# Gate build: a pair of PSUM buffers for each side's bit products, the j side's shared with the run-ahead products

## The chip, the cores and the metric

One core of a Trainium2 chip runs the whole program. The metric is the time of one execution in microseconds on the device, as the median of several runs.

## The reference

A two-layer backbone over 512 latent tokens and 256 context tokens, width 1024. Each layer has an attention part (mLSTM and differential attention in layer 0, windowed attention in layer 1) and then PEER, which is what this case is about: for each token and each of 8 heads, two lists of 128 scores are made, the 16 best of each are paired, the 16 best pairs pick 16 of 16384 single-neuron experts, and the token's output is the sum over the picked experts.

```python
s = jnp.einsum('nhpd,hpkd->nhpk', q, keys)
sv, si = lax.top_k(s, PEER_TOPK)                       # 16 best of 128, for both halves p
cand = sv[:, :, 0, :, None] + sv[:, :, 1, None, :]
cidx = si[:, :, 0, :, None] * PEER_NKEYS + si[:, :, 1, None, :]
cs, ci = lax.top_k(cand.reshape(n, PEER_HEADS, -1), PEER_TOPK)
gate = jax.nn.softmax(cs, axis=-1)
a = jnp.einsum('nd,nhkd->nhk', xt, u[eidx])
w = gate * jax.nn.gelu(a, approximate=False)
return jnp.einsum('nhk,nhkd->nd', w, v[eidx])
```

## The kernel before

PEER is done in two ways at once. For the three first blocks of 128 latent tokens (384 tokens) it is dense: a matrix of gates G[token, expert], zero where an expert is not picked, is built and stored to memory (`gd`). Then a loop over 128 slices `j` of 128 experts makes A = u x^T (tile `dA`), z = gelu(A) G and adds z^T v into six PSUM banks (`dacc`). For the other blocks (the fourth latent one, and the context's two) the picked rows of u and v are fetched by indirect DMA, one expert per token and step, and worked on by VectorE (lines 1023 and 1036). These gather steps are issued beside the dense work.

The stage around the change is the first half of `peer` (the block under `self.mixing()`), once in each layer:
- `route` makes queries (`pqps`) and scores (`pss`) on TensorE; `select` (lines 924 to 1001) finds the best pairs, a chain of many small VectorE instructions with steps on GpSimd (line 980) and ScalarE between them, for four blocks.
- After each of the first three blocks `gate_build` (from line 1062) runs: VectorE cuts the expert numbers i and j into bits (lines 1073 and 1075), which go through memory (`bd`) to come back transposed (`gbits`). Then 32 units per block, 96 per layer, one for every four tokens. `front`: two TensorE products of the bits, `gds` (line 1091), one for the i side and one for the j side, each in a PSUM bank of its own, are 1 exactly where all bits agree; ScalarE's Relu makes `ghot` of the i side (line 1097), VectorE's max and multiplication by the gate makes `ghot` of the j side (line 1095). `back`: four fp32 products `gps` (line 1108; eight records in the profile) make G for four tokens, and after two units ScalarE copies them to `gch` (line 1110). `pipe` calls `front` of a unit ahead of `back` of the one before.
- In layer 0, `mod(1, [0, 1])` makes two modulation rows for layer 1: 128 products `modps` (line 252), read by VectorE (lines 353 to 356).
- Then the first `dA` tiles of the dense loop run ahead, 18 in layer 0 and 27 in layer 1, with 24 products each (line 217). Their weights are split into a rounded and a remaining part: `whi` on ScalarE and `wlo` (line 196) on GpSimd and VectorE in turn. From the dense phase on the same work has the names `dhi` and `dlo`.

In layer 0, 48 gather steps belong to this stage (`GROWS`), three for every five units from the 17th on.

PSUM is divided among three tags with two buffers each: `pj` (`pqps`, `modps`, `dA` and others), `po` (`pss`, `gtp`, `gds`) of one bank a buffer, `big` (`gps`) of two. A buffer is given out in the order in which the program asks, and a user of it waits until the last readers of the buffer's previous user are done. The order of instructions on each engine is made by a scheduler when the program is built; it may put an instruction ahead of others that come earlier in the program, as far as the buffers allow it.

Of the kernel before, what the change touches and what calls it, by code (L numbers as in the profile page):

```python
# [110 lines left out]
class Kern:  # L111
# [951 lines left out]
    def gate_build(self, b, sel, alloc, beside):  # L1063

        nc, wk = self.nc, self.wk
        _, g, fij, _ = sel
        pl = alloc().bitcast(BF16).rearrange("p (e x) -> p e x", e=8)
        nc.gpsimd.memset(pl[:, 7, :], 1.0)  # L1070
        for s in range(2):
            bu = alloc().bitcast(U32).rearrange("p (e x) -> p e x", e=8)
            nc.vector.tensor_copy(bu[:, 7, :], fij[:, 128 * s:128 * s + 128])
            for e in range(7):
                nc.vector.tensor_scalar(bu[:, e, :], bu[:, 7, :], 1 << e, None, op0=OP.bitwise_and)
            nc.scalar.copy(pl[:, 0:7, 128 * s:128 * s + 128], bu[:, 0:7, :])
        nc.sync.dma_start(self.bd[b].rearrange("(t e) x -> t e x", e=8), pl)
        pt = self.po([128, 128], "gtp")
        nc.tensor.transpose(pt, g, self.ident)
        gT = wk.tile([128, 128], F32, name="gT", tag="gT", bufs=2)  # L1080
        nc.scalar.copy(gT, pt)
        bits, G, ps = {}, {}, {}

        def front(u):
            c, t0 = u
            if c % 4 == 0 and t0 == 0:
                bits[0] = wk.tile([128, 4, 256], BF16, name="gbits", tag="gbits", bufs=2)
                nc.sync.dma_start(bits[0], self.bd[b].rearrange("(c p) x -> p c x", p=128)[:, c:c + 4, :])
            d = [self.po([128, 4, 128], "gds") for _ in range(2)]
            for s in range(2):  # L1090
                nc.tensor.matmul(d[s], bits[0][:, c % 4, 128 * s:128 * s + 128], self.gB[:, t0:t0 + 4, :],  # L1091
                                 start=True, stop=True)
            h = [wk.tile([128, 4, 128], F32, name="ghot", tag="ghot", bufs=6) for _ in range(2)]
            t = 16 * c + t0
            i = nc.vector.scalar_tensor_tensor(h[1], d[1], 0.0, gT[:, t:t + 4].unsqueeze(2).broadcast_to([128, 4, 128]),
                                               op0=OP.max, op1=OP.mult)
            nc.scalar.activation(h[0], d[0], AF.Relu)
            return h + [i]

        def back(u, h):  # L1100
            c, t0 = u
            if t0 == 0:
                G[0] = wk.tile([128, 128, 16], F32, name="gch", tag="gch", bufs=2)
            if t0 % 8 == 0:
                ps[0] = self.big([128, 8, 128], "gps")
            beside(h[2])
            for t in range(4):
                nc.tensor.matmul(ps[0][:, t0 % 8 + t, :], h[0][:, t, :], h[1][:, t, :], start=True, stop=True)  # L1108
            if t0 % 8:
                nc.scalar.copy(G[0][:, :, t0 - 4:t0 + 4], ps[0].rearrange("p t j -> p j t"))  # L1110
            if t0 == 12:
                nc.scalar.dma_start(self.gd[8 * b + c], G[0])

        self.pipe([(c, t0) for c in range(8) for t0 in range(0, 16, 4)], front, back)

    def halves(self, src, shape, eng):
# [432 lines left out]
```

## Time and profile before

| | us |
|---|---|
| median of 3 runs | 4182.2 |
| lowest and highest | 4175.84, 4185.61 |
| the profiled execution | 4186.29 |
| its span in the trace | 4184.5 |

All times of the trace count from the start of the span. The stage of the change lies from 1099.8 (the last `pqps` product starts) to 1385.9 (the dense phase's first product) in layer 0, and from 2940 to 3215.8 in layer 1. Where a product stands in a timeline with "x8", eight of them are drawn together; TensorE's records overlap, so the rate is read from starts, not from durations.

### The profile page before, as it was taken

The numbers are of one execution on the slowest core, as the hardware profiler recorded it, in microseconds if no ns is written. First come the engines' busy times: TensorE is split into PE (matmuls) and PEld (weight loads), VectorE is DVE, ScalarE is ACT, GpSimd is POOL, SyncE is SP. The second block draws the span as 40 slices with busy tenths as digits, with TensorE's granted clock in tenths as the row PEclk, the third lists the DMA queues.
The fourth block names the chain that finished last, engine by engine and source line by source line (L and its number), as shares of the span: only waits on it lengthen the run. The fifth ranks groups of instructions, "written<-read, shape, count | busy, mean of one in ns | idle before, by whom it ended". The sixth has DMA issues, their size and how long they took to land.

```text
span 4184.5 us, 56313 instructions
## 1 busy us (share of the span) xinstructions
PE 3808.1 (91%) x19774; PEld 3252.5 (78%) x19780; DVE 3281.6 (78%) x5763; ACT 1526.5 (36%) x2798; POOL 2266.9 (54%) x1644
## 2 busy tenths in 40 slices
PE   8988777758899899999999889999999999999999
PEld 5776554546687799999889777777887899999987
DVE  4259888977988899999989987537955977777788
ACT  3322322412156433333333324332366333333333
POOL 1016767554453588778778563004531766666664
PEclk9999988878999999999999999999999999999999
DMA  5556888786339999989899995423346978788778
GB/s 193 171 201 207 314 316 308 263 314 234 129 121 371 361 326 346 350 310 343 317 332 331 341 332 194 154 90 112 117 161 241 347 275 285 275 288 278 280 266 314
DMA packets 389674, 1099.30 MB, mean 263 GB/s; under 512 B 32959, under 2 KB 140807, under 8 KB 383246
## 3 DMA queue, kind: packets, MB, share of 16 engines
q0 software_dynamic: 147456, 536.94, 35.4%
q1 hardware_dynamic: 232142, 497.95, 34.8%
q10 hardware_dynamic: 9792, 60.82, 3.5%
q8 instruction: 155, 2.54, 0.2%
q14 instruction: 129, 1.06, 0.1%
HBM read 1024.18 MB, written 71.40 MB: 262 GB/s over the span
## 4 chain that ended last, share of the span: by engine, by line
PE 55%; DMA 14%; DVE 13%; issue 10%; POOL 7%; ACT 2%; SPq 0%; POOLq 0%; ACTq 0%; DVEq 0%
PE dacc L1178 19%; PE dA L217 17%; DMA uv<-in_pr_u_dram,ix 4%; POOL uv L1010 4%; DMA uv<-in_pr_v_dram,ix 3%; PE pqps L217 2%; DMA draw<-in_uT_dram 2%; PE ops L223 2%; PE gps L1108 2%; DVE junkv L1023 2%; PE oo L1335 1%; PE gds L1091 1%; PE ops L1305 1%; PE modps L252 1%; PE vps L223 1%
## 5 line engine op out<-in xcount | busy, mean ns | idle before, releaser
L1178 PE MATMUL dacc<-dhi,dw 128*128 128x512 f32 x3072 | 986.6, 391 | 5.6 <-ACT dw L1171 3.8
L1010 POOL DMA_INDIRECT uv<-in_pr_u_dram,ix x512 | 670.2, 1309 | 463.0 <-DVE pa L1023 330.4
L1010 POOL DMA_INDIRECT uv<-in_pr_v_dram,ix x512 | 684.1, 1336 | 399.6 <-DVE pacc L1036 274.3
L1023 DVE CUSTOM_DVE_ANT_0 junkv<-uv,x 128x1024 bf16<-128x1024 f32 x512 | 695.1, 1358 | 60.1 <-DMA uv<-in_pr_u_dram,ix 55.9
L1036 DVE SCALAR_TENSOR_TENSOR pacc<-uv,pw,pacc 128x1024 f32<-128x1024 f32 x508 | 701.3, 1381 | 42.0 <-DMA uv<-in_pr_v_dram,ix 38.1
L1178 PEld LDWEIGHTS dacc<-dhi,dw 128*128 128x128 f32 x3072 | 578.5, 188 | 122.5 <-ACT dw L1171 4.5
L1123 POOL TENSOR_TENSOR dlo<-draw,dhi 128x1024 fp32r<-128x1024 f32 x210 | 542.3, 2583 | 211.4 <-ACT dhi L1122 207.7
L1122 ACT CAST dhi<-draw 128x1024 fp32r<-128x1024 f32 x467 | 489.5, 1050 | 445.2 <-issue 176.1
L1178 PE MATMUL dacc<-dlo,dw 128*128 128x512 f32 x1536 | 603.9, 393 | 7.2 <-DVE dlo L1123 7.2
L1168 DVE TENSOR_TENSOR dz<-dz,dG 128x384 f32<-128x384 f32 x256 | 406.5, 1601 | 79.0 <-ACT dz L1138 75.1
L1171 ACT CAST dw<-dz 128x384 fp32r<-128x384 f32 x256 | 131.4, 514 | 708.2 <-PE dacc L1178 690.3
L217 PE MATMUL dA<-xth,dhi 128*128 128x384 f32 x1688 | 335.3, 340 | 11.6 <-ACT dhi L1122 9.8
L1123 DVE TENSOR_TENSOR dlo<-draw,dhi 128x1024 fp32r<-128x1024 f32 x257 | 322.2, 1254 | 27.5 <-ACT dhi L1122 26.7
L1178 PEld LDWEIGHTS dacc<-dlo,dw 128*128 128x128 f32 x1536 | 289.1, 188 | 66.2 <-DVE dlo L1123 9.7
L217 PEld LDWEIGHTS dA<-xth,dhi 128*128 128x128 f32 x1688 | 306.5, 189 | 28.7 <-ACT dhi L1122 10.2
L217 PE MATMUL dA<-xtl,dhi 128*128 128x384 f32 x1688 | 327.4, 335 | 0.0
L217 PE MATMUL dA<-xth,dlo 128*128 128x384 f32 x1688 | 326.6, 334 | 0.8 <-POOL dlo L1123 0.8
L217 PEld LDWEIGHTS dA<-xtl,dhi 128*128 128x128 f32 x1688 | 296.7, 188 | 0.1
L217 PEld LDWEIGHTS dA<-xth,dlo 128*128 128x128 f32 x1688 | 295.6, 188 | 1.2 <-POOL dlo L1123 1.1
L1172 DVE TENSOR_TENSOR dw<-dz,dw 128x384 fp32r<-128x384 f32 x256 | 162.8, 636 | 151.5 <-ACT dw L1171 151.5
L1108 PEld LDWEIGHTS gps<-ghot 128*128 128x128 f32 x1536 | 202.2, 192 | 49.9 <-issue 21.9
L196 POOL TENSOR_TENSOR wlo<-wraw,whi 128x1024 fp32r<-128x1024 f32 x55 | 132.9, 2418 | 194.7 <-ACT whi L195 121.3
(341 smaller groups left out, 6044.9 us busy)
## 6 DMA issues: line engine op xcount, KB each, us to landing
draw<-in_pr_v_dram SPq DMA_DIRECT2D x256, 512.0 KB
draw<-in_uT_dram SPq DMA_DIRECT2D x211, 512.0 KB
wraw<-in_wb_dram SPq DMA_DIRECT2D x150, 512.0 KB
gd<-gch ACTq DMA_DIRECT2D x48, 1024.0 KB
dG<-gd SPq DMA_DIRECT2D x30, 1536.0 KB
wraw<-in_mod_t_dram SPq DMA_DIRECT2D x48, 512.0 KB
wraw<-in_uT_dram SPq DMA_DIRECT2D x45, 512.0 KB
wraw<-in_mod_w_dram SPq DMA_DIRECT2D x32, 512.0 KB
```

The source lines that it names most:

```text
L196: eng.tensor_tensor(lo, raw, hi.bitcast(F32), op=OP.subtract)
L217: self.nc.tensor.matmul(ps, w[wi][:, k, :], x[xi][:, k, 0:T], start=(i == 0), stop=(i == 23))
L1010: nc.gpsimd.indirect_dma_start(out=t, out_offset=None, in_=a[table], in_offset=bass.IndirectOffsetOnAxis(ap=ix[:, c:c + 1], axis=0))
L1023: nc.vector.tensor_tensor_reduce(out=junk, in0=u, in1=x, op0=OP.mult, op1=OP.add, scale=1.0, scalar=0.0, accum_out=A[:, c:c + 1])
L1036: nc.vector.scalar_tensor_tensor(acc, v, W[:, c:c + 1], acc, op0=OP.mult, op1=OP.add)
L1108: nc.tensor.matmul(ps[0][:, t0 % 8 + t, :], h[0][:, t, :], h[1][:, t, :], start=True, stop=True)
L1122: nc.scalar.copy(hi, raw)
L1123: eng.tensor_tensor(lo, raw, hi.bitcast(F32), op=OP.subtract)
L1168: nc.vector.tensor_tensor(z3, z3, self.G[:, :, j % JG, :], op=OP.mult)
L1171: nc.scalar.copy(wh, z)
L1172: i = nc.vector.tensor_tensor(wl, z, wh.bitcast(F32), op=OP.subtract)
L1178: self.nc.tensor.matmul(acc[b][:, h, :], w[wi][:, 128 * b:128 * b + 128], v[vi][:, 512 * h:512 * h + 512], start=(j == 0 and i == 0), stop ...
```

## The change

One line of `front`. Both `gds` of a unit came from the tag `po`, so a unit held both of its buffers. Now the i side's (`d[0]`) comes from `po` and the j side's (`d[1]`) from `pj`, with two buffers for each side.

```diff
         def front(u):
             c, t0 = u
...
-            d = [self.po([128, 4, 128], "gds") for _ in range(2)]
+            d = [self.po([128, 4, 128], "gds"), self.pj([128, 4, 128], "gds")]
             for s in range(2):
                 nc.tensor.matmul(d[s], bits[0][:, c % 4, 128 * s:128 * s + 128], self.gB[:, t0:t0 + 4, :],
                                  start=True, stop=True)
```

No instruction is added or taken away, but the scheduler's order changes on all engines. On TensorE in layer 0, behind the last queries, stood before (`gtp` is the transposition of the gates of block 0):

```order
L884 MATMUL pss<-ky,pq 128x128 x4
L252 MATMUL modps<-wraw,sc 2x128 x104
L217 MATMUL dA<-xth,whi 128x384 x8
L217 MATMUL dA<-xtl,whi 128x384 x8
L1079 MATMUL gtp<-cst,dgt 128x128
L217 MATMUL dA<-xth,whi 128x384 x8
L217 MATMUL dA<-xtl,whi 128x384 x8
L217 MATMUL dA<-xth,wlo 128x384 x16
```

...and further down, where the first two units' `gds` stand among the products of the fifth and sixth tile:

```order
L217 MATMUL dA<-xtl,whi 128x384 x5
L217 MATMUL dA<-xth,wlo 128x384 x3
L1091 LDWEIGHTS gbits
L1091 MATMUL gds<-gB,gbits 128x512
L1091 LDWEIGHTS gbits
L1091 MATMUL gds<-gB,gbits 128x512
L217 MATMUL dA<-xth,wlo 128x384 x5
L217 MATMUL dA<-xtl,whi 128x384 x3
L217 MATMUL dA<-xth,wlo 128x384 x8
L1091 LDWEIGHTS gbits
L1091 MATMUL gds<-gB,gbits 128x512
L1091 LDWEIGHTS gbits
L1091 MATMUL gds<-gB,gbits 128x512
L1108 MATMUL gps<-ghot 128x128 x4
```

In the same place, behind the last scores, stands now:

```order
L884 MATMUL pss<-ky,pq 128x128 x8
L1079 MATMUL gtp<-cst,dgt 128x128
L1091 LDWEIGHTS gbits
L1091 MATMUL gds<-gB,gbits 128x512
L1091 LDWEIGHTS gbits
L1091 MATMUL gds<-gB,gbits 128x512
L1091 LDWEIGHTS gbits
L1091 MATMUL gds<-gB,gbits 128x512
L1091 LDWEIGHTS gbits
L1091 MATMUL gds<-gB,gbits 128x512
L1091 LDWEIGHTS gbits
L1091 MATMUL gds<-gB,gbits 128x512
L1108 MATMUL gps<-ghot 128x128 x4
```

The `modps` and the `dA` products are gone from there: the first unit's `gds` follow the last scores at once, and five `gds` stand ahead of the first `gps` instead of four. The run of units goes on to the end of the gate build, where TensorE's rows now are:

```order
L1091 MATMUL gds<-gB,gbits 128x512
L252 MATMUL modps<-wraw,sc 2x128 x13
L1108 MATMUL gps<-ghot 128x128 x12
L252 MATMUL modps<-wraw,sc 2x128 x3
L1108 MATMUL gps<-ghot 128x128 x4
L252 MATMUL modps<-wraw,sc 2x128 x112
L217 MATMUL dA<-xth,whi 128x384 x8
L217 MATMUL dA<-xtl,whi 128x384 x8
L217 MATMUL dA<-xth,whi 128x384 x8
```

Here follow all 128 `modps` and then all 432 `dA` products of the 18 tiles (before, behind the last `gps` of this layer came the first `dhi` product). In layer 1, 42 `dA` products stand between the last three units' `gps`, and 606 behind them.

On VectorE, in layer 0, at the first units, the rows were these before (924 to 992 are the selection's lines, 1073 and 1075 the bits of the next block):

```order
L981 TENSOR_REDUCE sel<-sel 128x64
L1095 SCALAR_TENSOR_TENSOR ghot<-gds,gT 128x512
L988 TENSOR_SCALAR fij<-sel 128x64
L989 TENSOR_SCALAR fij<-fij 128x64
L990 TENSOR_SCALAR fij<-fij 128x64
L991 SCALAR_TENSOR_TENSOR sel<-fij,sel 128x64
L1073 CAST sel<-fij 128x128
L992 TENSOR_TENSOR sel<-sel 128x64
L1075 TENSOR_SCALAR sel<-sel 128x128 x3
L977 TENSOR_TENSOR sel<-sel,cst 128x1024
L1075 TENSOR_SCALAR sel<-sel 128x128 x4
L196 TENSOR_TENSOR wlo<-wraw,whi 128x1024
L1095 SCALAR_TENSOR_TENSOR ghot<-gds,gT 128x512
```

And now, some ten units into the gate build, with two blocks still to be selected (1023 is the gather step, `x_3582` its block of tokens):

```order
L988 TENSOR_SCALAR fij<-sel 128x64
L1095 SCALAR_TENSOR_TENSOR ghot<-gds,gT 128x512
L989 TENSOR_SCALAR fij<-fij 128x64
L1095 SCALAR_TENSOR_TENSOR ghot<-gds,gT 128x512
L1023 ISA junkv,pa<-uv,x_3582 128x1024
L1023 ISA pa 128x1
L990 TENSOR_SCALAR fij<-fij 128x64
L1095 SCALAR_TENSOR_TENSOR ghot<-gds,gT 128x512
L1023 ISA junkv,pa<-uv,x_3582 128x1024
L1023 ISA pa 128x1
L991 SCALAR_TENSOR_TENSOR sel<-fij,sel 128x64
L1073 CAST sel<-fij 128x128
```

The `ghot` of the j side and the gather steps stand between the selection's steps, where there was one `ghot` for every ten or more of them; 56 of the 96 `ghot` of layer 0 stand ahead of the selection's last row (line 996), against 11 before, and 46 of layer 1, against 12. The `wlo` and the `mrow` rows (lines 196 and 353 to 356) stand behind the last `ghot` of the layer. On SyncE's queue the loads of `wraw` for `modps` and `dA` stand behind the last `gbits` load; before, they were spread over the stage.

## Rows read from the trace of the kernel before

**Rows 1.** Page, part 1: busy time, share of the span, instructions of each engine
```profile
PE 3808.1 (91%) x19774; PEld 3252.5 (78%) x19780; DVE 3281.6 (78%) x5763; ACT 1526.5 (36%) x2798; POOL 2266.9 (54%) x1644
```

**Rows 2.** Timeline of TensorE, end of the gate build, both layers: start, us, instructions, [idle before]
```profile
1377.46 1.13 PE L1108 MATMUL gps<-ghot 128*128 128x128 f32 x8 [0.40 <-DVE ghot L1095]
1385.85 2.93 PE L217 MATMUL dA<-xth,dhi 128*128 128x384 f32 x8 [7.26 <-ACT dhi L1122]
...
3212.12 1.16 PE L1108 MATMUL gps<-ghot 128*128 128x128 f32 x8 [0.28 <-ACT ghot L1097]
3215.82 2.93 PE L217 MATMUL dA<-xth,dhi 128*128 128x384 f32 x8 [2.54 <-ACT dhi L1122]
```

**Rows 3.** Busy time by stretch, all engines
```profile
core 0: us, PE busy (x) PEld busy (x) DVE busy (x) ACT busy (x) POOL busy (x), PEclk, DMA share, GB/s
1099.80:1159.00 59.20, 48.80 (x363) 39.54 (x363) 51.67 (x231) 9.28 (x16) 19.86 (x19) 0.97 0.53 172
1159.00:1378.70 219.70, 200.91 (x1304) 171.35 (x1305) 181.74 (x426) 135.27 (x211) 97.21 (x96) 0.99 0.71 266
2940.00:2996.00 56.00, 50.19 (x281) 48.84 (x280) 50.42 (x223) 17.84 (x29) 30.27 (x22) 0.97 0.31 98
2996.00:3213.30 217.30, 208.68 (x1347) 180.61 (x1348) 128.60 (x332) 141.52 (x222) 58.03 (x54) 0.98 0.49 183
```

**Rows 4.** Groups of TensorE, 1099.8 to 1378.7, then 2940 to 3213.3
```profile
L1091 PE MATMUL gds<-gB,gbits 128*128 128x512 bf16 x189 | 63.3, 378 | 14.8 <-DVE ghot L1095 9.3 <-ACT ghot L1097 3.8
L252 PE MATMUL modps<-wraw,sc 128*2 128x128 f32 x256 | 30.0, 275 | 5.3 <-DMA wraw<-in_mod_t_dram 4.2 <-DVE mrow L356 1.1
...
L1091 PE MATMUL gds<-gB,gbits 128*128 128x512 bf16 x189 | 64.6, 381 | 4.5 <-DVE ghot L1095 3.9
```

**Rows 5.** Timeline of TensorE: shortest unit; a free tile; two steady units
```profile
1249.26 0.61 PE L1091 MATMUL gds<-gB,gbits 128*128 128x512 bf16 x2
1250.59 0.59 PE L1091 MATMUL gds<-gB,gbits 128*128 128x512 bf16 x2
...
1408.83 1.55 PE L217 MATMUL dA<-xth,dhi 128*128 128x384 f32 x8
1412.99 0.39 PE L1178 MATMUL dacc<-dhi,dw 128*128 128x512 f32 x1
...
3206.60 1.05 PE L1108 MATMUL gps<-ghot 128*128 128x128 f32 x8
3209.47 1.05 PE L1108 MATMUL gps<-ghot 128*128 128x128 f32 x8
```

**Rows 6.** Timeline of VectorE, last step of the bits of block 0, both layers
```profile
1156.82 1.97 DVE L1075 TENSOR_SCALAR sel<-sel 128x128 uint32<-128x128 uint32 x14
...
2993.76 1.97 DVE L1075 TENSOR_SCALAR sel<-sel 128x128 uint32<-128x128 uint32 x14
```

**Rows 7.** The same stretches, line 196 (`wlo`) alone: VectorE busy, GpSimd busy
```profile
1099.80:1159.00 59.20, 2.41 (x2) 4.81 (x2) 0.97 0.53 172
1159.00:1378.70 219.70, 13.29 (x7) 17.71 (x7) 0.99 0.71 266
2940.00:2996.00 56.00, 9.28 (x6) 11.96 (x5) 0.97 0.31 98
2996.00:3213.30 217.30, 11.00 (x8) 19.34 (x8) 0.98 0.49 183
```

**Rows 8.** Groups of VectorE, 1099.8 to 1396
```profile
L1095 DVE SCALAR_TENSOR_TENSOR ghot<-gds,gT 128x512 f32<-128x512 f32 x96 | 65.9, 686 | 26.6 <-PE gds L1091 26.6
L1023 DVE CUSTOM_DVE_ANT_0 junkv<-uv,x 128x1024 bf16<-128x1024 f32 x48 | 58.3, 1215 | 2.1 <-DMA uv<-in_pr_u_dram,ix 2.1
L354 DVE TENSOR_TENSOR mrow<-mrow,mg 2x256 f32<-2x256 f32 x4 | 5.2, 1300 | 3.6 <-DMA mg<-in_norm_g_dram 3.6
```

**Rows 9.** Timeline of TensorE, layer 1, after a wait for VectorE
```profile
3021.05 0.57 PE L1091 MATMUL gds<-gB,gbits 128*128 128x512 bf16 x1 [2.29 <-DVE ghot L1095]
3021.41 1.91 PE L1108 MATMUL gps<-ghot 128*128 128x128 f32 x8
```

## The prediction

> **What bounds the kernel now.** I read the page first. TensorE is busy for 91% of the span, VectorE for 78% [rows 1]; so work that TensorE has to do later is paid for, unless it was idle then. The change touches one stage, which occurs once in each of the two layers: expert selection and the building of the gates, before the dense phase. I looked for the edges of that stage in TensorE's timeline. In layer 0 the last gate product (`gps`) starts at 1377.5 us and the dense phase's first product at 1385.9; in layer 1 they start at 3212.1 and 3215.8 [rows 2]. The busy times by stretch show what the stage is made of [rows 3]. While the selection runs (1099.8 to 1159 and 2940 to 2996) VectorE is busy 51.7 of 59.2 us and 50.4 of 56.0; this chain of small instructions sets the pace. TensorE is nearly as busy there, 48.8 and 50.2 us, but with other work: the `modps` products (layer 0 only) and the run-ahead `dA` products, which depend neither on the selection nor on the gates. In the rest of the stage both engines are busy, TensorE 200.9 of 219.7 us in layer 0 and 208.7 of 217.3 in layer 1, VectorE 181.7 and 128.6. So now VectorE's selection and TensorE's run-ahead products cover each other, and the gate build comes after with most of its units.
>
> **What the change does to that.** The j side's `gds` now takes its buffer from the tag `pj`, which `modps` and `dA` use too. A tag has two buffers, handed out in the order in which the program asks. The program asks for 96 `gds` buffers per layer before it asks for `modps` and `dA`. Before, these were the only users of `pj` after the scores, so they ran ahead; now each waits until all but the last two `gds` of the layer have been read. The order listing shows it: in layer 0 all 128 `modps` and 432 `dA` products stand behind the gate build, all but the first 16 behind its last row; in layer 1 606 of 648 `dA` stand behind the last `gps`. The gate build moves forward in exchange: 56 of the 96 `ghot` of layer 0 now stand before VectorE's last selection step (11 before), 46 in layer 1 (12 before). Nothing else on TensorE changes place.
>
> **The small gain that the diff names.** A pair of banks for each side lets TensorE write the next unit's `gds` while both reads of the last are still under way. What it can remove is TensorE's idle time ahead of `gds`, 14.8 us in layer 0 and 4.5 in layer 1 [rows 4]: 19 us in all at the most. In steady state two units take 2.87 us, from one `gps` to the next but one [rows 5], so 1.435 us each; I keep that price, and take no gain here beyond the ends of the gate build worked out next.
>
> **Layer 0, end of the gate build.** VectorE finished the bits of block 0 at 1156.82 + 1.97 = 1158.8 us [rows 6]. Ahead of that stood 2.4 us of `wlo` subtractions [rows 7] and the `mrow` work of `modps`, 5.2 us with 3.6 us of waiting for its loads [rows 8]; all of that moves behind, so the bits are ready some 11 us sooner, at 1148. From 1159 to the end VectorE had 181.7 us of work, of which 13.3 were `wlo` [rows 3, 7]; 168.5 us remain, among them the 96 `ghot` (65.9 us) and the 48 gather steps (58.3 us) [rows 8], whose number stays. How densely can VectorE do this? It ran at 51.7/59.2 = 0.87 in the selection alone. Full density is the lower bound, 1316; the 181.7/219.7 = 0.83 of the later stretch gives 1352. I take 0.87, because most of the work is again selection with fillers: 1148 + 194 = 1342, against 1378.6 (the last `gps` row's start and its 1.13 us): 37 us sooner.
>
> **Layer 0, what comes behind.** The `modps` products: 30.0 us of TensorE and 5.3 us idle for their loads and evictions [rows 4], 35 us; nothing else is left to fill those 5 us. The `dA` products: 18 tiles of 24. Without a neighbour 24 take 4.16 us, from the first of them to the first `dacc` behind [rows 5], so 75 us; the loads, casts and subtractions for a tile are spread over four engines and were hidden at this rate in the dense phase, which I assume here too. Layer 0 loses 35 + 75 - 37 = 73 us.
>
> **Layer 1.** No `modps` and no gather steps here. Bits of block 0: 2993.76 + 1.97 = 2995.7 [rows 6], less 9.3 us of `wlo` ahead of them [rows 7]: 2987. VectorE's work from there was 128.6 less 11.0 [rows 3, 7], 117.6 us, of which 96 `ghot` at 686 ns [rows 8] are 66. Up to its last selection step it has 51.6 us of selection and 46 `ghot` (31.6 us), 83 us, at 50.4/56.0 = 0.90 92 us: 3079. The remaining 50 units are TensorE's, 1.435 us each, 72 us: the gates end at 3151, against 3213.3, 62 us sooner. Then 606 `dA` at 4.16/24 us, 105 us. Layer 1 loses 43 us.
>
> **The gaps ahead of the dense phase.** TensorE stood idle 7.3 us ahead of the dense phase's first product in layer 0 and 2.5 in layer 1, for a cast that waits for its load [rows 2]. With the gates written out long before, and fewer transfers beside it, these loads can come earlier, or stay where they are if their buffers are freed by the last `dA`. Bounds: 0 and 10 us off; I take 8 off, since the DMA share falls from the 0.71 of layer 0's stretch [rows 3].
>
> **Sum.** 73 + 43 - 8 = 108 us. The profiled execution took 4186.3 us, its span 4184.5; the median of the runs is 4182.2, a tenth of a per cent less, and I add to the median: 4290 us.
>
> **The clock, row and rule.** In layer 1 TensorE waited 2.29 us for a `ghot`; the eight `gps` records behind it took 1.91 us instead of 1.05 [rows 5, 9], the lower of its two levels (1.2 and 2.4 GHz). Such waits will be common once TensorE has only gates to do during the selection. The Trainium skill, page "TensorE: Matmul & The Clock Gate", section "Why this matters for your kernels", says that idle gaps between matmul bursts make TensorE fall back to half clock; that speaks against this change. The row agrees. By the row alone I charge nothing in the sum, since a slow unit still fits between two `ghot` of the selection; by the rule taken for every unit of the selection it would be the rival below that costs 41 us more.
>
> **Rivals.**
> First, the other side: faster. If `modps` and `dA` found idle time again, or the gate build gained more than they lose, only the 19 us of idle time would count: about 4163. For that the gates of layer 0 would have to end 110 us sooner than now, at 1268; VectorE has 168.5 us of work after 1148 and could not be done before 1316. The order listing rules out the first way. 2 in 100. No change at all needs the same, 2 in 100.
> Second, a much smaller loss: VectorE without a wait (25 us in layer 0, 9 in layer 1), units at 1.33 us (the shortest distance from one pair of `gds` to the next [rows 5]; 5 us), both gaps gone (2 us more): about 4249; a few per cent of the rest of the loads hidden would bring it under 4240. For it speaks that `ghot` now fills VectorE's waits for GpSimd. 14 in 100 for less than 4240.
> Third, the clock: the 102 units that stand in the selection at 2.6 us instead of 1.44 (scaled by 1.91/1.05), where VectorE gives one about every 2.2 us in layer 0: 0.4 us each, 41 us, 4331. It decides from the point at which a unit at the low level is longer than VectorE's spacing. Together with VectorE at 0.83 (10 us in each layer) it leaves the range upward. 12 in 100 above 4335.
> Fourth, `dA` alone behind the gates runs at its loads and not at TensorE: at 5 us a tile, 45 tiles cost 38 us more, 4328. Against it: the same tiles ran at 4.16 us in the dense phase under more transfers. It lies within the range.
>
> **Range.** The forecast and what lies around it: 70 in 100, 4240 to 4335, which leaves 12 above and 18 below (14, 2 and 2). Faster by over 0.2% 0.02, within 0.2% (about what a measurement of this kernel can tell from no change, 8 us) 0.02, slower 0.96.
>
> **What the profile after would show.** In both layers no `dA` from the tag `pj` before the last few `gps`; TensorE's busy share in the selection down to a third or so; the last `gps` near 1342 in layer 0; then an unbroken run of some 35 us `modps` and 75 us `dA`; the dense phase from about 1455 (70 us later) and 110 us later in layer 1. Wrong would be the forecast if the gate build ended over 60 us sooner in layer 0, if `dA` ran in its gaps, or if the dense phase, unchanged in its order, became shorter by itself.

## The result and the profile after

The changed kernel took 4275.5 us (median of four runs, 4270.5 to 4279.4) and the kernel before 4180.5 (four runs): the ratio is 1.0223, 95% interval 1.0208 to 1.0238, 95 us more. Ratios, here and below, are those on record, worked out from single executions; they can differ by 0.1% from the quotient of the medians (here 1.0227). The forecast was 4290, its range 4240 to 4335.

The profiled execution took 4279.4 us with a span of 4277.6. The page's first part, against [rows 1]: no engine got noticeably more work, the shares fell.

```profile
PE 3812.9 (89%) x19744; PEld 3253.8 (76%) x19780; DVE 3262.2 (76%) x5763; ACT 1528.4 (36%) x2798; POOL 2237.2 (52%) x1644
```

TensorE is busy for 5 us more and the span is 93 us longer, so about 88 us of the loss are time in which TensorE now stands idle. Where, is seen in the busy times by stretch, with the columns of [rows 3]. The first three rows of layer 0 end where the first block's bits, the last gate product and the last `modps` end; in layer 1 the rows are selection alone, gate build, run-ahead tiles:

```profile
core 0: us, PE busy (x) PEld busy (x) DVE busy (x) ACT busy (x) POOL busy (x), PEclk, DMA share, GB/s
1099.80:1147.00 47.20, 6.03 (x24) 4.58 (x22) 40.94 (x225) 3.12 (x9) 14.57 (x16) 0.54 0.00 1
1147.00:1331.40 184.40, 150.89 (x977) 119.37 (x996) 170.25 (x421) 104.27 (x162) 76.45 (x90) 0.91 0.76 284
1331.40:1368.40 37.00, 27.52 (x226) 19.06 (x225) 4.54 (x11) 2.06 (x2) 0.00 (x0) 0.95 0.71 248
1368.40:1445.60 77.20, 75.14 (x433) 74.82 (x433) 11.93 (x9) 38.08 (x55) 21.47 (x9) 1.00 0.41 133
...
2995.40:3042.50 47.10, 4.89 (x19) 3.67 (x17) 41.79 (x220) 3.33 (x9) 15.59 (x17) 0.53 0.05 19
3042.50:3203.90 161.40, 144.00 (x990) 117.56 (x1009) 109.72 (x323) 107.72 (x168) 34.61 (x47) 0.97 0.48 188
3203.90:3311.80 107.90, 104.63 (x605) 104.31 (x603) 14.70 (x12) 51.97 (x77) 28.62 (x13) 1.00 0.41 136
```

TensorE worked 48.8 of the first 59.2 us before [rows 3]; now it has 6 us of work in 47. The work that it had there is found in the third and fourth row, where VectorE has almost nothing to do (4.5 of 37.0 and 11.9 of 77.2 us). The second row is the gate build, which now runs beside the selection. The timeline of TensorE at its end, layer 0 and then layer 1, answers to [rows 2]:

```profile
1330.28 1.16 PE L1108 MATMUL gps<-ghot 128*128 128x128 f32 x8
1331.37 1.91 PE L252 MATMUL modps<-wraw,sc 128*2 128x128 f32 x16
...
1340.70 7.36 PE L252 MATMUL modps<-wraw,sc 128*2 128x128 f32 x64 [2.48 <-DMA wraw<-in_mod_t_dram]
...
1363.36 3.65 PE L252 MATMUL modps<-wraw,sc 128*2 128x128 f32 x32 [1.70 <-DMA wraw<-in_mod_t_dram]
1368.37 1.66 PE L217 MATMUL dA<-xth,whi 128*128 128x384 f32 x8 [1.36 <-ACT whi L195]
...
1441.98 1.55 PE L217 MATMUL dA<-xth,wlo 128*128 128x384 f32 x8
1445.59 1.66 PE L217 MATMUL dA<-xth,dhi 128*128 128x384 f32 x8 [2.06 <-ACT dhi L1122]
...
3202.39 0.83 PE L1108 MATMUL gps<-ghot 128*128 128x128 f32 x6
...
3306.94 1.55 PE L217 MATMUL dA<-xth,wlo 128*128 128x384 f32 x8
3311.76 2.55 PE L217 MATMUL dA<-xth,dhi 128*128 128x384 f32 x8 [3.27 <-ACT dhi L1122]
```

After the last `gps` comes what used to run ahead of it: all but 16 of the 128 `modps`, with waits for their loads, then 18 `dA` tiles without a gap, then the dense phase's first product (`dhi`). In layer 1 the last `gps` stands at 3202.4 and the tiles end at 3308.5.

To compare kernels whose earlier parts start a few us apart, I measure the stage from the start of the last `pqps` product to the start of the first `dhi` product, and the dense phase from there to the start of the last `dacc`; each is a difference of two starts in TensorE's timeline of the profiled execution, in us. In the kernel before, that last `pqps` product starts at 1099.5 and 2939.9.

| | layer 0: last `gps` | stage | dense | layer 1: last `gps` | stage | dense |
|---|---|---|---|---|---|---|
| before | 278.8 | 286.4 | 1004.2 | 273.1 | 275.9 | 958.1 |
| after | 230.2 | 344.6 | 1001.2 | 207.8 | 316.4 | 955.3 |
| difference | -48.6 | +58.2 | -3.0 | -65.3 | +40.5 | -2.8 |

The four differences of stages and dense phases make +92.9 us; the spans differ by 93.1.

### The profile page after: what moved, and what is told of

Read it like the earlier page. It is cut to its first block, busy times and chain, and to the rows that moved or that the text cites. A ratio compares the mean times of both kernels' runs of the same rounds, so it can differ in the third digit from the quotient of the medians.

```text
span 4277.6 us, 56312 instructions
## 1 busy us (share of the span) xinstructions
PE 3812.9 (89%) x19744; PEld 3253.8 (76%) x19780; DVE 3262.2 (76%) x5763; ACT 1528.4 (36%) x2798; POOL 2237.2 (52%) x1644
## 4 chain that ended last, share of the span: by engine, by line
PE 57%; DVE 16%; DMA 11%; issue 8%; POOL 6%; ACT 1%; SPq 0%; POOLq 0%; ACTq 0%; DVEq 0%; another core or an unknown queue 0%
PE dA L217 20%; PE dacc L1178 18%; POOL uv L1010 4%; DMA uv<-in_pr_u_dram,ix 3%; PE ops L223 3%; DMA uv<-in_pr_v_dram,ix 2%; PE pqps L217 2%; DVE junkv L1023 2%; PE gps L1108 2%; DMA draw<-in_uT_dram 2%; PE modps L252 1%; PE oo L1335 1%; DVE ghot L1095 1%; DVE pacc L1036 1%; DVE dz L1168 1%
## 5 line engine op out<-in xcount | busy, mean ns | idle before, releaser
L1010 POOL DMA_INDIRECT uv<-in_pr_v_dram,ix x512 | 674.4, 1317 | 406.2 <-DVE pacc L1036 273.9
L1168 DVE TENSOR_TENSOR dz<-dz,dG 128x384 f32<-128x384 f32 x256 | 418.7, 1649 | 75.8 <-ACT dz L1138 75.8
```

The lines of the kernel that those rows point to most:

```text
L1010: nc.gpsimd.indirect_dma_start(out=t, out_offset=None, in_=a[table], in_offset=bass.IndirectOffsetOnAxis(ap=ix[:, c:c + 1], axis=0))
L1168: nc.vector.tensor_tensor(z3, z3, self.G[:, :, j % JG, :], op=OP.mult)
```

## The experiments

**Theory A** is the prediction's: the loss comes from the place in which the tag `pj` is handed out, which puts `modps` and `dA` behind the gate build, where they cover nothing. Its rivals B to E place it elsewhere or weigh a part of it differently; what each of them expects stands with each run. The questions were: is each layer's share what A says; does the loss follow the shared tag or the second pair; does it go when the same products are asked for earlier; and what is a run-ahead tile worth ahead of the gates and behind them.

### One layer at a time

The j side's `gds` come from `pj` in layer 0 only, or in layer 1 only (`1` in place of `0`):

```diff
-            d = [self.po([128, 4, 128], "gds"), self.pj([128, 4, 128], "gds")]
+            d = [self.po([128, 4, 128], "gds"), (self.pj if self.layer == 0 else self.po)([128, 4, 128], "gds")]
...
         upre = self.upre = UPRE[l]
+        self.layer = l
```

> The j side's gds take the tag pj in layer 0 alone. Theory A (order: the loss is the run-ahead products that now stand behind the gate build, less what the gate build ends sooner): the loss of layer 0 alone, 55 to 60 us, so 4236 us, plus or minus 6. Theory B (the gate build itself becomes slower, whatever happens to the run-ahead products: its VectorE part crowds the selection and TensorE falls to its lower clock): about half of the 95 us, in proportion to 96 units in each layer, 4228 us. Alone it doesn't tell them apart; with the next run it shows whether the two layers add up.

> The j side's gds take the tag pj in layer 1 alone. Theory A: 27 dA tiles (112 us) behind, gates some 62 us sooner, 40 us slower than before, 4220 us, plus or minus 6; together with the run for layer 0 it gives the 95 us. Theory B: as in layer 0, 47 us, 4228 us.

Layer 0 alone: 4227.4 us against 4181.9, ratio 1.0109 (1.0092 to 1.0126), 45.5 us. Layer 1 alone: 4219.4, 1.0093 (1.0076 to 1.0110), 37.5 us. Layer 1 is as A expected. Layer 0 lies below A's range and on B's figure, so the time alone decides nothing there. By the trace the changed stage of layer 0 is 53.6 us longer (340.0) and that of layer 1 41.2 (317.0), the unchanged ones 1.7 and 3.6 shorter; the stages bear A out, and what the time of the first run gives back lies outside them, in a dense phase of 997.3 us instead of 1004.2. Why it is shorter stays open. Together the two runs lose 83 us, 12 less than the changed kernel; the intervals of the three ratios allow that the layers simply add up (1.09% and 0.93% against 2.23%).

### Sharing without a second pair, and a second pair without sharing

Both sides from `pj`, so that a unit holds both buffers of the tag, as it did those of `po` before:

```diff
-            d = [self.po([128, 4, 128], "gds"), self.pj([128, 4, 128], "gds")]
+            d = [self.pj([128, 4, 128], "gds") for _ in range(2)]
```

> Both sides' gds take the tag pj, so there is one pair of buffers for a unit as before, and the sharing with the run-ahead products as after. Theory A: the order is that of the changed kernel, so the whole loss stays, 4275 us, and up to 10 us more since the second pair's run-ahead of gds is gone: 4275 to 4290 us. Theory B (it is the second pair that lets the gate build crowd the selection): most of the loss goes, 4180 to 4220 us.

4289.8 us, ratio 1.0264 (1.0247 to 1.0281). The whole loss is there without the second pair, and 14 us more (1.0264 against 1.0223), within A's range and far from B's. The groups of TensorE in the gate build of layer 0, first of this kernel (1091 to 1328 us), then of the changed one (1101 to 1331.4); behind the bar stand busy time, mean ns, then the idle time ahead and what ended it (18 of the 192 records of `gds` are missing from the trace of the changed kernel, so its busy times are not compared):

```profile
L1108 PE MATMUL gps<-ghot 128*128 128x128 f32 x768 | 105.5, 282 | 0.7 <-DVE ghot L1095 0.7
L1091 PE MATMUL gds<-gB,gbits 128*128 128x512 bf16 x192 | 68.6, 395 | 47.4 <-DVE ghot L1095 25.5 <-DMA gbits<-bd 15.2 <-ACT ghot L1097 4.9
```

```profile
L1108 PE MATMUL gps<-ghot 128*128 128x128 f32 x768 | 112.3, 294 | 21.9 <-DVE ghot L1095 20.7 <-ACT ghot L1097 0.5 <-ACT gch L1110 0.3
L1091 PE MATMUL gds<-gB,gbits 128*128 128x512 bf16 x174 | 57.5, 403 | 20.3 <-DMA gbits<-bd 15.4 <-ACT ghot L1097 1.8 <-DVE ghot L1095 1.5
```

With the order fixed, the second pair does what its words say: TensorE's wait ahead of `gds` for a `ghot` of VectorE falls from 25.5 to 1.5 us. But 20.7 us of waiting for `ghot` come up ahead of `gps` instead, since VectorE sets the pace; the last `gps` comes 4.8 us sooner in layer 0 and 7.4 in layer 1.

The other way round, the j side gets a tag of its own, for which the banks are freed by giving `gps` one-bank buffers (`gq`), with ScalarE's copy after every unit instead of every two:

```diff
-            d = [self.po([128, 4, 128], "gds"), self.pj([128, 4, 128], "gds")]
+            d = [self.po([128, 4, 128], "gds"), self.ps.tile([128, 4, 128], F32, name="gds", tag="pk", bufs=2)]
...
-            if t0 % 8 == 0:
-                ps[0] = self.big([128, 8, 128], "gps")
+            ps[0] = self.ps.tile([128, 4, 128], F32, name="gps", tag="gq", bufs=2)
...
-                nc.tensor.matmul(ps[0][:, t0 % 8 + t, :], h[0][:, t, :], h[1][:, t, :], start=True, stop=True)
-            if t0 % 8:
-                nc.scalar.copy(G[0][:, :, t0 - 4:t0 + 4], ps[0].rearrange("p t j -> p j t"))
+                nc.tensor.matmul(ps[0][:, t, :], h[0][:, t, :], h[1][:, t, :], start=True, stop=True)
+            nc.scalar.copy(G[0][:, :, t0:t0 + 4], ps[0].rearrange("p t j -> p j t"))
```

> The j side has its own pair of PSUM banks, shared with nothing; the room comes from gps, which here has one bank a unit instead of two banks for two units, so ScalarE copies G after every unit. Theory A: the run-ahead products stand again among the units, the loss goes: 4165 to 4190 us, since at most the 19 us of TensorE's idle time ahead of gds can be won. Theory B (the second pair makes the gate build slower): 4230 to 4275 us.

4160.4 us, ratio 0.9958 (0.9941 to 0.9975): the pair is there, the sharing is not, and the loss is gone. By the medians this kernel is 21 us faster than the one before, by the ratio 18, and faster than A expected (4165 to 4190). Its control has the `gps` edit alone, on the kernel before:

> The kernel before with one PSUM bank of gps for each unit and a copy of G after every unit, both sides' gds still in po, two banks unused: the part of e4_own_banks that is not the second pair. Theory A says that e4's gain of 21 us (4160 us) comes from the second pair, so this run is as fast as before, 4176 to 4192 us. Rival C: the smaller gps tiles are what gained there, 4160 to 4170 us.

4171.0 us (eleven runs), ratio 0.9977 (0.9968 to 0.9985). So 9 of the 21 us come from the one-bank `gps` buffers, more than A expected of them and just under what rival C did. The rest, 12 us by the medians and 8 by the ratios, would be the pair's; the two intervals overlap (0.9968 to 0.9975), so this part is not shown clear of noise. TensorE's group of `gps` in the kernel before (1099.8 to 1378.7 us), then the groups of the kernel with banks of its own, layer 0, 1098.8 to 1377 us:

```profile
L1108 PE MATMUL gps<-ghot 128*128 128x128 f32 x768 | 102.0, 276 | 0.7 <-DVE ghot L1095 0.6
```

```profile
L1107 PE MATMUL gps<-ghot 128*128 128x128 f32 x768 | 102.6, 282 | 6.3 <-ACT ghot L1097 2.3 <-ACT gch L1108 2.3 <-DVE ghot L1095 1.2
L1091 PE MATMUL gds<-gB,gbits 128*128 128x512 bf16 x192 | 60.0, 384 | 9.6 <-DVE ghot L1095 6.7 <-ACT ghot L1097 2.2 <-issue 0.4
```

Of the 14.8 us ahead of `gds` [rows 4] 9.6 are left, and 5.6 us more stand ahead of `gps` than before (0.7). The two waits together are as long as before. In the profiled execution, 29.7 us faster than that of before, the stages are 8.3 and 6.8 us shorter (278.1 and 269.1), mostly because the last `gps` comes 3.3 and 6.3 us sooner and the time from the start of the last `gps` to the dense phase in layer 0 shrank from 7.5 to 2.5. The dense phases are 7.0 and 4.0 shorter (997.2 and 954.1). Against the control's own profile (stages 283.9 and 268.9, dense phases 1001.5 and 954.2) what the pair adds in these two executions lies all in layer 0, 5.8 us in the stage and 4.2 in the dense phase; for the second I have no cause.

### The order mended by asking earlier

Tags as in the changed kernel, but the program now asks for `modps` and `dA` between the units. A step is one `dA` tile or one of the eight `modps` buffers (`mod_steps` is `mod` with a `yield` behind each); 13 steps of layer 0 (12 of layer 1) are asked for ahead of the first unit, then one at every fourth (third) unit:

```diff
+LEAD, EVERY = (13, 12), (4, 3)
...
         def front(u):
             c, t0 = u
+            self.fill()
...
+                def run_ahead():
+                    if l == 0:
+                        yield from self.mod_steps(1, [0, 1])
+                    for j in range(upre):
...
+                        z[j] = self.dense_u(j, u, self.pj([128, ND], "dA"), xt)
+                        yield
+                work, units = run_ahead(), [0]
+                def fill():
+                    for _ in range(LEAD[l] if units[0] == 0 else units[0] % EVERY[l] == 0):
+                        next(work, None)
+                    units[0] += 1
```

> The changed kernel, but modps and the dA tiles are asked for between the units: 13 of these steps (12 in layer 1) ahead of the first unit of block 0, then one ahead of every fourth unit (third in layer 1). The j side's gds still share the tag pj with them. Theory A (the loss is the place of the products in the order in which the tag is given out, nothing in the banks themselves): the loss goes and the gain of the second pair stays, 4150 to 4175 us. Theory D (gds and the run-ahead products in one tag hold each other up, wherever they stand: a dA holds a buffer for 4 us, in which the j side has only one): about half of the loss stays, 4210 to 4240 us.

4182.4 us against 4180.4, ratio 1.0004 (0.9993 to 1.0015). The loss of 95 us is gone with the same two pairs and the same shared tag; the gain on top that A expected (4150 to 4175) did not come. The control has the same asking and both sides from `po`, as before:

> The same interleaved asking, but both sides' gds in po as in the kernel before. Theory A: the tag pj already let these products run ahead, the order on TensorE is almost that of before, so 4176 to 4190 us. If e6 is faster than this run by 10 us or more, the second pair is worth that by itself; if the two are equal, it is worth nothing and any gain is that of the asking.

4177.4, ratio 0.9997 (0.9989 to 1.0006). The second pair is worth nothing here that the runs can tell. The two kernels' groups of TensorE, layer 0, show what its gain turned into; the first fence is the one with two pairs (1096 to 1380 us), the second the control (1098 to 1380); line 1098 is `gds` and line 1115 `gps`:

```profile
L1115 PE MATMUL gps<-ghot 128*128 128x128 f32 x768 | 104.7, 282 | 14.7 <-DVE ghot L1102 12.4 <-ACT ghot L1104 1.0 <-ACT gch L1117 0.9
L1098 PE MATMUL gds<-gB,gbits 128*128 128x512 bf16 x192 | 58.5, 380 | 7.1 <-DVE ghot L1102 3.8 <-ACT dz L1143 1.8 <-ACT ghot L1104 0.9
```

```profile
L1115 PE MATMUL gps<-ghot 128*128 128x128 f32 x768 | 101.3, 275 | 1.6 <-DVE ghot L1102 1.5
L1098 PE MATMUL gds<-gB,gbits 128*128 128x512 bf16 x192 | 64.2, 378 | 14.7 <-DVE ghot L1102 7.6 <-ACT ghot L1104 5.5
```

The pair takes 7.6 us from the wait ahead of `gds`, and 13 us appear ahead of `gps`, again for `ghot`. A denser asking makes no difference:

```diff
-LEAD, EVERY = (13, 12), (4, 3)
+LEAD, EVERY = (16, 15), (3, 2)
```

> As e6, with more of the run-ahead work early: 16 steps (15) ahead of the first unit, then one ahead of every third unit (second). Theory A: TensorE's idle time in the selection is filled sooner, but VectorE has more wlo work ahead of the first bits; within 8 us of e6. If the loss grows again by more, the place of single tiles matters, and then the first units are what counts.

4184.3, ratio 1.0010 (1.0002 to 1.0019), 2 us from the sparser one.

### What a run-ahead tile is worth on either side

Only eight tiles run ahead in each layer, in the changed kernel and in the one before; the 10 and 19 others fall to the dense phase:

```diff
-UPRE = 18, 27
+UPRE = 8, 8
```

> The changed kernel with 8 run-ahead dA tiles in each layer instead of 18 and 27; the other 10 and 19 are made in the dense phase. Theory A: after the change these tiles have no cover, a tile costs the same 4.2 us in either place, so nothing changes against the changed kernel: 4268 to 4282 us. Theory E (they still fill idle time of the gate build or of the start of the dense phase): slower than the changed kernel by more than 10 us.

> The kernel before with 8 run-ahead dA tiles in each layer. Theory A: there the tiles were covered by the selection. 29 tiles of 4.16 us, 121 us, lose it; the gate build ends sooner by as much as it was behind them on TensorE, by the sums of the prediction (37 and 62 us for all tiles, a bit over half of them here) some 55 us: 4180 + 65, 4230 to 4265 us. Theory E: the tiles had no cover before either, 4175 to 4195 us.

On the changed kernel: 4262.0 us against 4176.3, ratio 1.0201 (1.0184 to 1.0218). Taking 29 tiles away from behind the gates and adding them to the dense phase gains 9 us by the medians, or nothing (1.0201 against 1.0223, with overlapping intervals; 4262.0 lies 6 us below A's range). In the dense phase they cost the same or less, so they cover nothing where the change put them. On the kernel before: 4210.9, ratio 1.0077 (1.0060 to 1.0093), 34.6 us more. There the run-ahead tiles are worth something, though less than the 121 us of TensorE that 29 tiles at 4.17 us take, and less than A expected (4230 to 4265). The stages show both: layer 1's becomes 77.3 us shorter on the changed kernel and 53.3 on the one before, and the dense phase 77.7 and 75.7 longer; layer 0's 44.4 and 26.7 shorter, and the dense phase 30.1 and 27.3 longer. So in layer 0 ten tiles more in the dense phase take only 3 us each, in both kernels, and on the kernel before they are worth nothing ahead of the gates (26.7 against 27.3): what the tiles taken away are worth there lies in layer 1. Of the 31.8 us between the profiled spans the stages and dense phases hold 23; 7.6 lie ahead of the stage of layer 0, which begins that much later in this trace, and I have no cause for them.

The stretch behind the gates in layer 0 of the changed kernel with eight tiles, in the columns of busy times by stretch:

```profile
1332.50:1403.50 71.00, 61.32 (x419) 52.31 (x418) 10.33 (x15) 19.57 (x27) 9.56 (x4) 0.98 0.60 203
```

71 us for `modps` and eight tiles: the 37 us of `modps` and 8 x 4.17 make 70, the price that 18 tiles had.

## Why the prediction was right

**The order.** The step "each now waits until all but the last two `gds` of the layer have been read" is what the trace shows: no `dA` from `pj` stands before the last units. That this is the cause, and not the second pair, is shown by the kernel with both sides in `pj` (whole loss, no pair), the one with banks of its own (pair, no loss) and the one that asks earlier (same banks, no loss).

**Layer 0, end of the gate build** is the term that was mis-sized: 37 us sooner forecast, 48.6 measured. The bits of block 0 came as forecast, at 1146.9 (forecast 1148), from the timeline of VectorE; [rows 6] answer to it:

```profile
1144.95 1.98 DVE L1075 TENSOR_SCALAR sel<-sel 128x128 uint32<-128x128 uint32 x14
```

From there the work was as counted, 170.3 us against 168.5, but VectorE did it at 170.25/184.4 = 0.92 and not at 0.87. The 0.87 was read from a stretch before in which VectorE stood idle for 7.5 us. Of these, 4.7 belonged to the `mrow` steps, which move behind (3.6 of them, the wait for `mg`, the forecast had already taken off ahead of the bits, so they count twice), and only 2.6 to waits for GpSimd. That it fits the selection alone in the changed kernel too, 40.94/47.20 = 0.87 with 5.9 us of waits for GpSimd, is luck. What it missed is the gate build: the selection's steps there wait for GpSimd for 0.2 us, where they waited 7.0 before, since `ghot` and gather steps now stand in these waits. The second rival had this mechanism. VectorE's waits (us in all, times, longest), before at 1099.8 to 1159 and at 1159 to 1378.7, then in the changed kernel at 1147 to 1331.4:

```profile
DVE mrow L354 <- DMA mg<-in_norm_g_dram: 3.6, 3, 2.2
DVE fij L981 <- POOL sel L980: 2.6, 1, 2.6
...
DVE sel L981 <- POOL sel L980: 3.6, 2, 1.9
DVE fij L981 <- POOL sel L980: 3.4, 2, 1.7
...
DVE sel L981 <- POOL sel L980: 0.2, 1, 0.2
```

The groups of VectorE, layer 0 (1099.8 to 1455) and then layer 1's `ghot` (2996 to 3204):

```profile
L1095 DVE SCALAR_TENSOR_TENSOR ghot<-gds,gT 128x512 f32<-128x512 f32 x96 | 64.7, 682 | 12.4 <-PE gds L1091 5.9 <-PE gps L1108 4.2 <-remote 0.8
L1023 DVE CUSTOM_DVE_ANT_0 junkv<-uv,x 128x1024 bf16<-128x1024 f32 x48 | 64.2, 1338 | 0.1
...
L1095 DVE SCALAR_TENSOR_TENSOR ghot<-gds,gT 128x512 f32<-128x512 f32 x96 | 64.4, 685 | 40.7 <-PE gds L1091 29.2 <-PE gps L1108 8.9 <-ACT gT L1081 1.6
```

The wait ahead of `ghot` fell from 26.6 us [rows 8] to 12.4; the gather steps wait for nothing any more, but one takes 1338 ns instead of 1215. In layer 1, where there are no gather steps to fill in, 40.7 us of waiting are left, most of it for `gds`.

**Layer 1, end of the gate build**: 62 us sooner forecast, 65.3 measured, and that this is so near is partly luck. The bits came as forecast, and the last selection step (line 996) starts at 3123.5. The stretches from the bits to it, and from there to the last `gps`, in the columns of busy times by stretch:

```profile
3042.50:3123.50 81.00, 65.77 (x441) 51.92 (x451) 75.89 (x272) 51.60 (x85) 29.55 (x44) 0.94 0.42 166
3123.50:3203.45 79.95, 77.78 (x549) 65.19 (x557) 33.83 (x51) 55.71 (x83) 5.07 (x4) 1.00 0.53 209
```

Up to that step VectorE sets the pace, at 75.9/81.0 = 0.94 and not the 0.90 taken, so the step comes 11 us sooner than forecast (128 us behind the last `pqps`, not 139). From there TensorE sets it, as forecast, but the remaining 50 units take 80 us and not 72: the 42 `dA` products that stand between the last three units, about 7 us at 4.16/24 each, were counted neither there nor behind the gates.

**What comes behind.** `modps` took 37.0 us (forecast 35), with 27.5 of work and 9.5 of waiting where 30.0 and 5.3 were counted, the tiles stand from 1368.4 to 1443.5, 75 us (forecast 75, 4.17 us each), and in layer 1 the 606 products fill 104.6 of 107.9 us (forecast 105). The tiles were not bound by their loads; the fourth rival's 5 us did not occur.

**The gaps** ahead of the dense phase went from 7.3 to 2.1 us and from 2.5 to 3.3 [rows 2], 4.5 us off where 8 were taken. TensorE's busy share in the selection fell to 0.13 and 0.10 until the first bits, and to 0.57 and 0.55 for the whole of it up to its last step (97.0 of 169.1 us in layer 0, 70.7 of 128.1 in layer 1), where the forecast looked for a third or so.

**The dense phases** became 3 us shorter each, which the forecast had named as something that would speak against it. They are 0.6 to 8.9 us shorter than in the profile of before in every kernel with the same number of tiles ahead, the control with the old banks too, and the profiled execution of before (4186.3 us) was itself 5.8 above its median; a cause was not settled.

**The sum**: 108 forecast; -12 and -3 for the gate ends, +2 for `modps`, +4 for the gaps, -6 for the dense phases, makes 93, the difference of the spans. So the path and the terms were those of the forecast; the largest error is the density of VectorE in layer 0, and the errors of layer 1's gate build nearly cancel.

**The clock.** The price of the slow units was left out of the sum, and the gate build of layer 0 ended sooner than forecast even so. The timeline of TensorE at the start of layer 0's gate build:

```profile
1137.62 0.47 PE L1079 MATMUL gtp<-cst,dgt 128*128 128x128 f32 x1 [23.65 <-POOL dgt L1001]
1153.47 0.61 PE L1091 MATMUL gds<-gB,gbits 128*128 128x512 bf16 x1 [15.38 <-DMA gbits<-bd]
...
1155.58 1.92 PE L1108 MATMUL gps<-ghot 128*128 128x128 f32 x8
...
1159.61 1.05 PE L1108 MATMUL gps<-ghot 128*128 128x128 f32 x8
...
1165.18 2.03 PE L1108 MATMUL gps<-ghot 128*128 128x128 f32 x8 [2.65 <-DVE ghot L1095]
```

After 23.7 and 15.4 us idle (granted clock 0.54 in the stretch 1099.8 to 1147) the first eight `gps` took 1.92 us, and 2.03 after another 2.65 us idle, against 1.05 in between. The granted clock was 0.50 and 0.51 under the two slow ones (1153.5 to 1157.2 and 1165.2 to 1167.2) and 1.00 under the fast one (1159.6 to 1160.7): the lower and the upper of the two levels. In the whole gate build `gps` took 112.3 us instead of the 102.0 of the same group before, 10 us, in a stretch where VectorE was busy for 92%; the third rival's 41 us, with every unit of the selection slow, did not come. The Trainium skill, page "TensorE: Matmul & The Clock Gate", section "Why this matters for your kernels", warns of falling back to half clock after idle gaps; the trace agrees with that (1.92 against 1.05 us). What the 10 us cost the kernel, beside a VectorE that was nearly always busy, no run shows by itself.

## What to carry to other kernels

Buffers of one tag are handed out here in program order, so a tag that an early user shares with work meant to run ahead turns that work into work that runs behind. Before giving a tag a new user, ask where in the program its other users ask for it, and which engine's waiting they fill; here TensorE worked 48.8 of 59.2 us of the selection on them. What such cover is worth has to be measured: ten tiles of layer 0 were worth nothing there. A second buffer gains little where the wait that it removes comes up again one product later: TensorE waited for `ghot` ahead of `gds` with one pair, and ahead of `gps` with two.

The version that beats both kernels is the one with tags of their own for the j side and for one-bank `gps` buffers: 4160.4 us, 0.4% under the kernel before.

## What the runs showed that I had not expected

- One-bank `gps` buffers, with 192 copies by ScalarE instead of 96, are 9 us faster (0.9977) than two-bank ones with copies of twice the size. In the profiled executions, which are 20.0 us apart, the stages hold 9.5 of it (2.5 and 7.0) and the dense phases 6.6; why the smaller copies help was not tested.
- VectorE, with two independent streams to choose from, reached 0.92 busy in layer 0's gate build, where the selection alone ran at 0.87, before and after.
- Ten tiles added to layer 0's dense phase of the changed kernel cost 3.0 us each and not 4.17; nineteen added to layer 1's cost 4.1.
